# Two query blocks multiplied tile by tile at a kernel's start, with their weights loaded in another order

## The chip, the cores and the metric

The kernel runs on one core of a Trainium2 chip. The time is the device time of one execution in microseconds (us). The engines are TensorE (PE, matrix products), VectorE (DVE), ScalarE (ACT), GpSimd (POOL) and SyncE (SP, which issues the loads). Each works through its own instructions in order and waits for the others by semaphores.

## The reference

Two layers of a small transformer on 512 tokens with 1024 features, in float32. Only the beginning of the first layer is touched:

```python
a = rmsnorm(h, ln_mix_pre[layer])          # h = x at first
mem_n = rmsnorm(mem, ln_mem[layer])
proj = a @ w_in_a[layer]
u = proj[..., :MAIN_WIDTH]                  # 768 columns
v = proj[..., MAIN_WIDTH:2 * MAIN_WIDTH]    # 768 columns
q_mem = proj[..., 2 * MAIN_WIDTH:]          # 256 columns: the query blocks
...
mixed = concatenate([main, memory_attention(q_mem, mem_n, w_mem_kv[layer])], axis=-1)
h = h + rmsnorm(mixed @ w_out[layer], ln_mix_post[layer])
f = rmsnorm(h, ln_ffn_pre[layer])
f = (silu(f @ w_ffn_gate[layer]) * (f @ w_ffn_up[layer])) @ w_ffn_down[layer]
h = h + rmsnorm(f, ln_ffn_post[layer])
```

`rmsnorm(x, g)` divides a token by the root of its mean square and multiplies by the gains g.

## The kernel before

Activations lie with features on the 128 partitions and the 512 tokens along the row, so x is eight tiles, k = 0 to 7, each 128 features x 512 tokens (256 KB). To keep float32 accuracy every operand is cut into two parts: ACT writes a rounded first part ("hi"), DVE the remainder ("lo"), and a product is three matrix products, hi·hi, hi·lo and lo·hi. `split` (line 239) does this for weights, `scaled_parts` (lines 243 and 244) for activations, where it multiplies by the gains as well. `mm3` (lines 191 to 193) issues the three products. The division by the root mean square comes after the products, since it is one number for each token.

`layer_a` opens the program. SP's queue loads weights and x; `query_weights(m, c0, c1)` loads and cuts columns c0 to c1 of query block m's weights (a row of 1024 columns holds the block's eight 128 x 128 tiles, so a half of 512 columns, 256 KB, serves four tiles of x); `tokens(k0, k1)` loads tiles k0 to k1 - 1 of x and cuts them. The query products, two blocks m of 8 tiles with 3 products each, 48 in all, go into one PSUM accumulator for each block (`outs`). They are followed by the products of the first value block (`value_block`, names `v`), whose 128 x 256 accumulators are scaled by `evacuate` (ACT) as they finish.

Beside them runs the mean square: ACT squares each tile (`Norm.add`), DVE adds the squares into `acc`, PE sums over the partitions (`st`, line 288), DVE adds a constant (`var`), POOL takes the power -1/2 (`r`, line 260), and PE spreads it over the partitions (`rb`, line 257), whence DVE copies it to `rbc`. The squares are held back until the last tile of x is cut (`last_a`, `behind`).

Before all this PE runs ten products of zeros (`idle`). The order in which each engine runs the instructions is set by a scheduler from the order of the code and the dependencies; it can move an instruction past others of its engine. SP's loads keep the order of the code. A load also waits until an earlier one, eight before it at most, has landed (its semaphore is used again), and until its buffer is free.

Names in the listings below: `ahi_118`, `alo_119` are the two parts of tile 0 of x, `120`/`121` those of tile 1, and so on to `132`/`133` of tile 7. `ps_183` and `ps_184` are the accumulators of query blocks 0 and 1. `whi`/`wlo` are parts of weights: 138/139 and 160/161 the two halves of block 0; for block 1 they are 155/156 and 175/176 before, 146/147 and 165/166 after; 235 to 250 are value weights.

## Time and profile before

| | us |
|---|---|
| median of 3 runs | 1107.92 (1107.33 to 1109.67) |
| profiled execution | 1106.27 |
| its span, first to last instruction | 1104.4 |
| PE busy in the span | 1096.5 (99%) |
| DVE, ACT, POOL busy | 887.5 (80%), 679.6 (62%), 25.2 (2%) |

The profile comes from one execution. Its timeline lists instructions by engine with their start, duration, line, operation, output and inputs; a bracket at the end names the idle time before an instruction and what ended it. Instructions that follow each other closely can be merged in a row (x2). PE's durations overlap, since products are pipelined, so the distance of two starts tells the rate.

### The profile page before, as it was taken

What the parts mean: (1) busy time and instruction counts of PE and PEld (TensorE: products, weight loads), DVE (VectorE), ACT (ScalarE), POOL (GpSimd) and SP (SyncE); (2) the same over time, 40 slices, a digit from 0 to 9 for tenths busy, and PEclk for the clock granted to TensorE, in tenths of its full rate; (3) what the DMA queues carried; (4) which work ended last, traced back from release to release, by engine and by line L of the source; (5) the groups of instructions that cost most, each with busy time, mean ns of one, the idle gap of its engine ahead of it and who ended that gap; (6) DMA issues with size and microseconds to landing.
All of it is one profiled execution on the core that took longest, in us unless ns stands there. A gap on an engine that the chain in (4) does not pass through costs nothing.

```text
span 1104.4 us, 19436 instructions
## 1 busy us (share of the span) xinstructions
PE 1096.5 (99%) x7332; PEld 998.5 (90%) x7332; DVE 887.5 (80%) x1751; ACT 679.6 (62%) x1426; POOL 25.2 (2%) x41
## 2 busy tenths in 40 slices
PE   9999999999999999999999999999999999999998
PEld 7998889999899899998988998889999899899996
DVE  7879759997698498797968789868998698588776
ACT  7776578664365254477647788868665266255454
POOL 0000000000000000001000000000000000000000
PEclk9999999999999999999999999999999999999999
DMA  7521331334135133245222655531225134233222
GB/s 269 160 79 58 115 115 39 115 115 138 54 115 147 56 104 116 77 154 174 77 77 59 150 129 131 148 115 39 77 91 158 58 114 132 61 114 117 77 96 76
DMA packets 64020, 118.63 MB, mean 107 GB/s; under 512 B 5236, under 2 KB 40072, under 8 KB 63928
## 3 DMA queue, kind: packets, MB, share of 16 engines
q1 hardware_dynamic: 63032, 116.57, 34.8%
q8 instruction: 57, 0.93, 0.4%
q0 software_dynamic: 192, 0.52, 0.2%
q10 hardware_dynamic: 704, 0.32, 0.1%
q14 instruction: 35, 0.29, 0.1%
HBM read 105.23 MB, written 2.10 MB: 97 GB/s over the span
## 4 chain that ended last, share of the span: by engine, by line
PE 93%; ACT 3%; DVE 2%; issue 1%; DMA 0%; SPq 0%; POOLq 0%; POOL 0%; DVEq 0%; ACTq 0%
PE y L191 10%; PE y L192 10%; PE y L193 10%; PE a L191 5%; PE a L193 5%; PE a L192 5%; PE ps L191 4%; PE ps L192 4%; PE ps L193 4%; PE e L191 3%; PE e L193 3%; PE e L192 3%; PE x L193 3%; PE x L191 3%; PE x L192 3%; PE v L191 2%
## 5 line engine op out<-in xcount | busy, mean ns | idle before, releaser
L239 ACT CAST whi<-raw 128x512 fp32r<-128x512 f32 x460 | 277.4, 620 | 262.1 <-PE y L193 118.5
L239 DVE TENSOR_TENSOR wlo<-raw,whi 128x512 fp32r<-128x512 f32 x460 | 307.2, 689 | 112.4 <-ACT whi L239 110.3
L191 PE MATMUL y<-whi,fhi 128*128 128x512 f32 (+1 forms) x356 | 139.6, 393 | 0.0
L193 PE MATMUL y<-whi,flo 128*128 128x512 f32 (+1 forms) x356 | 139.4, 391 | 0.0
L192 PE MATMUL y<-wlo,fhi 128*128 128x512 f32 (+1 forms) x356 | 139.3, 391 | 0.0
L193 PE MATMUL x<-xshi,wlo 128*128 128x256 f32 x320 | 89.8, 281 | 0.0
L191 PE MATMUL x<-xshi,whi 128*128 128x256 f32 x320 | 89.7, 280 | 0.0
L191 PE MATMUL a<-xshi,whi 128*128 128x256 f32 x320 | 89.7, 281 | 0.0
L192 PE MATMUL a<-xslo,whi 128*128 128x256 f32 x320 | 89.7, 280 | 0.0
L192 PE MATMUL x<-xslo,whi 128*128 128x256 f32 x320 | 89.7, 280 | 0.0
L193 PE MATMUL a<-xshi,wlo 128*128 128x256 f32 x320 | 89.6, 281 | 0.0
L193 PEld LDWEIGHTS y<-whi,flo 128*128 128x128 f32 x356 | 66.9, 188 | 15.6 <-DVE flo L239 0.2
L192 PEld LDWEIGHTS y<-wlo,fhi 128*128 128x128 f32 x356 | 66.9, 188 | 14.8 <-DVE wlo L239 0.2
L191 PEld LDWEIGHTS y<-whi,fhi 128*128 128x128 f32 x356 | 66.9, 188 | 14.7
L191 PE MATMUL ps<-xshi,whi 128*128 128x256 f32 (+1 forms) x224 | 68.4, 305 | 0.0
L192 PE MATMUL ps<-xslo,whi 128*128 128x256 f32 (+1 forms) x224 | 66.7, 298 | 0.0
L193 PE MATMUL ps<-xshi,wlo 128*128 128x256 f32 (+1 forms) x224 | 66.3, 298 | 0.0
L191 PEld LDWEIGHTS a<-xshi,whi 128*128 128x128 f32 x320 | 60.3, 188 | 0.3
L192 PEld LDWEIGHTS a<-xslo,whi 128*128 128x128 f32 x320 | 60.2, 188 | 0.4
L191 PEld LDWEIGHTS x<-xshi,whi 128*128 128x128 f32 x320 | 60.2, 188 | 0.0
L193 PEld LDWEIGHTS x<-xshi,wlo 128*128 128x128 f32 x320 | 60.2, 188 | 0.0
L193 PEld LDWEIGHTS a<-xshi,wlo 128*128 128x128 f32 x320 | 60.2, 188 | 0.0
(296 smaller groups left out, 3077.5 us busy)
## 6 DMA issues: line engine op xcount, KB each, us to landing
raw<-in_w_gate SPq DMA_DIRECT2D x44, 512.0 KB, 3.6
raw<-in_w_up SPq DMA_DIRECT2D x44, 512.0 KB, 3.6
raw<-in_w_down SPq DMA_DIRECT2D x44, 512.0 KB, 3.9
raw<-in_w_out SPq DMA_DIRECT2D x16, 512.0 KB, 4.4
raw<-in_w_b_q SPq DMA_DIRECT2D x8, 512.0 KB, 4.6
raw<-in_w_a_v SPq DMA_DIRECT2D x6, 512.0 KB, 8.3
raw<-in_w_a_u SPq DMA_DIRECT2D x6, 512.0 KB
raw<-in_w_v SPq DMA_DIRECT2D x6, 512.0 KB, 3.6
```

What stands on the lines that cost most here:

```text
L191: PE.matmul(o, w[0], x[0], start=start, stop=False, skip_group_check=more)
L192: PE.matmul(o, w[0], x[1], start=False, stop=False, skip_group_check=more)
L193: return PE.matmul(o, w[1], x[0], start=False, stop=stop, skip_group_check=more)
L239: last_parts[:] = A.copy(hi, src), (eng or V).tensor_sub(lo, src, hi)
```

## The change

The code loads block 1's first half of weights between tile 0 and tile 1 of x instead of behind tile 3, and both second halves ahead of tiles 4 to 7 (block 1's stood behind tile 7). The products run over the tiles on the outside and the two blocks on the inside, where they ran over halves, then blocks, then the half's four tiles. The three products of a tile and block come in another order: those with the activation's first part come first, and its remainder last.

```diff
         query_weights(0, 0, 512)
-        for k in range(4):
+        tokens(0, 1)
+        query_weights(1, 0, 512)
+        for k in range(1, 4):
             tokens(k, k + 1)
-        query_weights(1, 0, 512)
-        query_weights(0, 512, 1024)
+        for m in range(2):
+            query_weights(m, 512, 1024)
         tokens(4, 6)
         tokens(6, 8)
         last_a = tuple(last_parts)
-        query_weights(1, 512, 1024)
...
             outs = [ps(t) for t in ("mm", "lg")]
-            for half in range(0, KT, 4):
+            for k in range(KT):
                 for o, w in zip(outs, wq):
-                    for k in range(half, half + 4):
-                        mm3(o, w[k], a[k], k == 0, k == KT - 1)
+                    PE.matmul(o, w[k][0], a[k][0], start=k == 0, stop=False)
+                    PE.matmul(o, w[k][1], a[k][0], start=False, stop=False)
+                    PE.matmul(o, w[k][0], a[k][1], start=False, stop=k == KT - 1)
```

The numbers of instructions on each engine stay the same. PE's order differs from before among the 48 query products and at one place behind them, ACT's and DVE's in the first 60 instructions or so, SP's in the first eight; everything later stands in the order of before.

PE, the first twelve query products, before:

```order
L191 MATMUL ps_183<-ahi_118,whi_138 128x512
L192 MATMUL ps_183<-alo_119,whi_138 128x512
L193 MATMUL ps_183<-ahi_118,wlo_139 128x512
L191 MATMUL ps_183<-ahi_120,whi_138 128x512
L192 MATMUL ps_183<-alo_121,whi_138 128x512
L193 MATMUL ps_183<-ahi_120,wlo_139 128x512
L191 MATMUL ps_183<-ahi_122,whi_138 128x512
L192 MATMUL ps_183<-alo_123,whi_138 128x512
L193 MATMUL ps_183<-ahi_122,wlo_139 128x512
L191 MATMUL ps_183<-ahi_124,whi_138 128x512
L191 MATMUL ps_184<-ahi_118,whi_155 128x512
L192 MATMUL ps_183<-alo_125,whi_138 128x512
```

PE at the same place now:

```order
L672 MATMUL ps_183<-ahi_118,whi_138 128x512
L673 MATMUL ps_183<-ahi_118,wlo_139 128x512
L672 MATMUL ps_184<-ahi_118,whi_146 128x512
L674 MATMUL ps_183<-alo_119,whi_138 128x512
L672 MATMUL ps_183<-ahi_120,whi_138 128x512
L673 MATMUL ps_184<-ahi_118,wlo_147 128x512
L674 MATMUL ps_184<-alo_119,whi_146 128x512
L673 MATMUL ps_183<-ahi_120,wlo_139 128x512
L674 MATMUL ps_183<-alo_121,whi_138 128x512
L672 MATMUL ps_184<-ahi_120,whi_146 128x512
L673 MATMUL ps_184<-ahi_120,wlo_147 128x512
L674 MATMUL ps_184<-alo_121,whi_146 128x512
```

The twelve products took tiles 0 to 3 for block 0 and one of block 1; now they are all of tiles 0 and 1, for both blocks, and the third of them needs block 1's weights.

ACT, from its first cut on, before (135 and 136 are the raw weights of blocks 0 and 1):

```order
L239 CAST whi_138<-raw_135 128x512
L243 ACTIVATE ahi_118<-h,gains 128x512
L243 ACTIVATE ahi_120<-h,gains 128x512
L243 ACTIVATE ahi_122<-h,gains 128x512
L243 ACTIVATE ahi_124<-h,gains 128x512
L239 CAST whi_155<-raw_136 128x512
L239 CAST whi_160<-raw_135 128x512
L243 ACTIVATE ahi_126<-h,gains 128x512
L243 ACTIVATE ahi_128<-h,gains 128x512
L243 ACTIVATE ahi_130<-h,gains 128x512
L243 ACTIVATE ahi_132<-h,gains 128x512
L239 CAST whi_175<-raw_136 128x512
```

ACT at the same place now:

```order
L239 CAST whi_138<-raw_135 128x512
L243 ACTIVATE ahi_118<-h,gains 128x512
L239 CAST whi_146<-raw_136 128x512
L243 ACTIVATE ahi_120<-h,gains 128x512
L243 ACTIVATE ahi_122<-h,gains 128x512
L243 ACTIVATE ahi_124<-h,gains 128x512
L239 CAST whi_160<-raw_135 128x512
L239 CAST whi_165<-raw_136 128x512
L243 ACTIVATE ahi_126<-h,gains 128x512
L243 ACTIVATE ahi_128<-h,gains 128x512
L243 ACTIVATE ahi_130<-h,gains 128x512
L243 ACTIVATE ahi_132<-h,gains 128x512
```

The cut of block 1's first half moved ahead of tiles 1 to 3, that of its second half ahead of tiles 4 to 7. DVE's remainders follow in the same order.

PE in the second value tile (`v_301`), around the sums of squares `st_314`, before:

```order
L192 MATMUL v_301<-wlo_246,ahi_128 128x256
L288 MATMUL st_314<-avg,acc_266 128x1 x4
L193 MATMUL v_301<-whi_245,alo_129 128x256
L191 MATMUL v_301<-whi_249,ahi_130 128x256
L192 MATMUL v_301<-wlo_250,ahi_130 128x256
L193 MATMUL v_301<-whi_249,alo_131 128x256
L191 MATMUL v_301<-whi_249,ahi_132 128x256
L192 MATMUL v_301<-wlo_250,ahi_132 128x256
```

PE at the same place now:

```order
L192 MATMUL v_301<-wlo_246,ahi_128 128x256
L193 MATMUL v_301<-whi_245,alo_129 128x256
L191 MATMUL v_301<-whi_249,ahi_130 128x256
L192 MATMUL v_301<-wlo_250,ahi_130 128x256
L193 MATMUL v_301<-whi_249,alo_131 128x256
L191 MATMUL v_301<-whi_249,ahi_132 128x256
L192 MATMUL v_301<-wlo_250,ahi_132 128x256
L288 MATMUL st_314<-avg,acc_266 128x1 x4
```

The sums moved behind six value products; the spread `rb` twelve and more products further on kept its place.

## The prediction

> **What bounds the kernel now.** I read the page's first lines, then the waits of TensorE (PE) after the opening, then the opening itself, engine by engine, in the timeline. All times are microseconds from the span's start.

> ```profile
> span 1104.4 us, 19436 instructions
> PE 1096.5 (99%) x7332; PEld 998.5 (90%) x7332; DVE 887.5 (80%) x1751; ACT 679.6 (62%) x1426; POOL 25.2 (2%) x41
> ```

> PE is busy in 99% of the span. Busy alone says little, so the next view lists what PE waited for from 18 us to the end (releaser, us in total, times, longest):

> ```profile
> PE o L532 <- ACT pT L239: 0.5, 1, 0.5
> PE yt L881 <- ACT yg L866: 0.2, 1, 0.2
> PE mo L493 <- DVE pT L239: 0.2, 1, 0.2
> PE tr L464 <- DVE p L457: 0.2, 1, 0.2
> PE o L532 <- DVE pT L239: 0.2, 1, 0.2
> ```

> These are all of them: 1.3 us in 1086. After the opening PE never waits for a load, so a shift of PE's stream at 18 us goes through to the end nearly one to one. What the change can win or lose is therefore decided before the first value product. PE's opening:

> ```profile
> 1.26 4.45 PE L89 MATMUL idle<-zeros 128*128 128x512 bf16 x10 [1.26 <-DVE zeros L81]
> 5.78 0.80 PE L191 MATMUL ps<-ahi,whi 128*128 128x512 f32 x1
> 6.56 0.60 PE L192 MATMUL ps<-alo,whi 128*128 128x512 f32 x1
> 7.00 0.40 PE L193 MATMUL ps<-ahi,wlo 128*128 128x512 f32 x1
> 7.43 0.50 PE L191 MATMUL ps<-ahi,whi 128*128 128x512 f32 x1
> 8.22 0.50 PE L192 MATMUL ps<-alo,whi 128*128 128x512 f32 x1 [0.28 <-DVE alo L244]
> 8.55 0.40 PE L193 MATMUL ps<-ahi,wlo 128*128 128x512 f32 x1
> 8.79 0.39 PE L191 MATMUL ps<-ahi,whi 128*128 128x512 f32 x1
> 9.11 0.50 PE L192 MATMUL ps<-alo,whi 128*128 128x512 f32 x1
> 9.45 0.39 PE L193 MATMUL ps<-ahi,wlo 128*128 128x512 f32 x1
> 9.68 0.63 PE L191 MATMUL ps<-ahi,whi 128*128 128x512 f32 x2
> 10.14 0.40 PE L192 MATMUL ps<-alo,whi 128*128 128x512 f32 x1
> 18.76 0.28 PE L191 MATMUL v<-whi,ahi 128*128 128x256 f32 x1
> 18.88 0.28 PE L192 MATMUL v<-wlo,ahi 128*128 128x256 f32 x1
> ```

> The first column is the start. The 48 query products begin at 5.78; the twelfth starts at 10.14, and the first value product at 18.76, so the last 37 run without a gap at (18.76 - 10.14) / 37 = 0.233 us each. Without any wait 48 of them would take 11.18 us and end at 16.96: the opening holds 1.8 us of waiting and slow running, which is 0.16% of the time. No rearrangement of these 48 products alone can win more than that. A change of 0.2%, 2.2 us, is about what a measurement of this kernel tells from none.

> **What the opening waits for.** ScalarE (ACT) makes the first part of each tile; its rows, with the wait in brackets:

> ```profile
> 4.41 0.62 ACT L239 CAST whi<-raw 128x512 fp32r<-128x512 f32 x1 [1.67 <-DMA raw<-in_w_a_q]
> 5.00 0.72 ACT L243 ACTIVATE ahi<-h,gains 128x512 fp32r<-128x512 f32 x1
> 6.65 0.72 ACT L243 ACTIVATE ahi<-h,gains 128x512 fp32r<-128x512 f32 x1 [0.93 <-DMA h<-in_x]
> 7.55 1.38 ACT L243 ACTIVATE ahi<-h,gains 128x512 fp32r<-128x512 f32 x2 [0.17 <-DMA h<-in_x]
> 8.88 1.28 ACT L239 CAST whi<-raw 128x512 fp32r<-128x512 f32 x2
> 10.79 1.34 ACT L243 ACTIVATE ahi<-h,gains 128x512 fp32r<-128x512 f32 x2 [0.64 <-DMA h<-in_x]
> 12.49 1.34 ACT L243 ACTIVATE ahi<-h,gains 128x512 fp32r<-128x512 f32 x2 [0.36 <-DMA h<-in_x]
> 13.73 0.60 ACT L239 CAST whi<-raw 128x512 fp32r<-128x512 f32 x1
> 7.41 2.31 DVE L244 SCALAR_TENSOR_TENSOR alo<-h,gains,ahi 128x512 fp32r<-128x512 f32 x3 [0.90 <-ACT ahi L243]
> 1.00:5.00 4.00, 3.74 (x9) 1.35 (x10) 1.20 (x6) 2.07 (x3) 1.12 (x3) 1.00 0.76 215
> 5.00:10.00 5.00, 4.61 (x13) 2.11 (x12) 3.89 (x6) 3.86 (x7) 0.00 (x0) 1.00 0.95 333
> 10.00:15.00 5.00, 5.00 (x23) 4.04 (x22) 4.42 (x8) 4.01 (x8) 0.00 (x0) 1.00 1.01 395
> ```

> The loads come in the order of SP's queue. Tile 0 is there by 5.00, tile 1 lands at 6.65, tile 2 at 7.55, tile 3 by 8.2 (the pair at 7.55 has no gap), the two halves of weights by 8.88 and 9.5, tiles 4-5 at 10.79, tiles 6-7 at 12.49. The last three rows are stretches of the span, which end in granted clock, DMA share and GB/s. From 10 to 15 us the share is 1.01 at 395 GB/s: the loads are the limit, and a 256 KB piece put ahead of others delays them by 262 KB / 395 GB/s = 0.66 us.

> **The change part by part.** *Block 1's first half (256 KB) goes from sixth place in the queue to third.* Pieces of the same size change places: I give the half tile 1's landing, 6.65, tile 1 that of tile 2, 7.55, tile 2 that of tile 3, 8.2. ACT then cuts the half from 6.65 to 7.27, tile 1 from 7.55 to 8.27; VectorE (DVE) follows 0.75 us behind (three in 2.31), tile 1 done at about 9.05.

> *PE's order.* The first two products (tile 0, both parts of block 0's weights) can run at 5.78 and 6.21. The third needs the half's first part: 7.33, with the 0.06 us that lay between ACT's end (7.37) and PE (7.43) for tile 1. The fourth follows; the fifth needs tile 1's first part, 8.33; the sixth to eighth follow at the 0.23 to 0.33 us of the rows 8.22 to 8.79, to 9.05; the ninth needs tile 1's remainder, ready at 9.12. I put the ninth at 9.28. From there 40 products x 0.233 = 9.33 us: the value products start at 18.61, against 18.76: **-0.15 us**. The saved waits for tiles 2 and 3 are paid by the longer wait for the half and for tile 1: one tile now gives six products, but arrives a place later. If tile 1 came as early as before, the ninth would start at 8.25 and the sum would be -1.2 us; if the half and tile 1 came a further 0.66 us late, the ninth would start at 9.94 and it would be +0.5. I take the middle, since the places are of equal size.

> *Both second halves go ahead of tiles 4 to 7* (one was there already, the other moves past two loads of 512 KB on SP's queue). Tiles 4-5 land 0.66 us later, 11.45, and tiles 6-7 at 13.15. The second cut's 0.62 us on ACT fits into the wait for tiles 4-5 (0.64 before, longer now); without that cover it would delay them 0.62 us. PE asks for tile 4 at product 25: 9.28 + 16 x 0.233 = 13.01, and ACT has it at 11.45 + 0.72 = 12.17. For tile 6, product 37, it is 15.81 against 13.9. Both are hidden, by 0.8 and 1.9 us: 0. The cut at 13.73 is gone, so ACT starts the squares right after tile 7, at 13.15 + 1.34 = 14.5, instead of after that cut, at 14.3: the last add comes about 0.2 us later. No other loads, GpSimd work or instruction counts change; the order beyond 40 us is the same.

> *The column sums move on PE*, by six value products, as the rows of the part on the change show; the diff doesn't say it. What hangs on them:

> ```profile
> 19.04 4.88 DVE L277 TENSOR_TENSOR acc<-acc,sq 128x512 f32<-128x512 f32 x7
> 23.62 0.95 PE L288 MATMUL st<-avg,acc 128*128 128x1 f32 x8
> 24.61 0.16 DVE L291 TENSOR_SCALAR var<-st 128x4 f32<-128x4 f32 x1 [0.68 <-PE st L288]
> 24.85 1.41 POOL L260 TENSOR_TENSOR r<-var,mhalf 128x4 f32<-128x4 f32 x1 [21.92 <-DVE var L291]
> 26.29 0.84 ACT L641 ACTIVATE vg<-v,r 128x256 f32<-128x256 f32 x2 [1.96 <-POOL r L260]
> 26.77 0.60 PE L257 MATMUL rb<-ident,r 128*128 128x128 f32 x4
> ```

> The sums (st) go through DVE (var) and GpSimd (r), and the next step on PE is the spread of r (rb), whose place stays. r is there at 26.29 and PE reaches rb at 26.77, so rb has 0.48 us to spare. Six products at 0.12 us (18.76 to 18.88) are 0.71 us: st starts at 23.62 + 0.71 - 0.15 = 24.18 and r comes at 26.85, while PE, 0.15 us ahead, is at rb at 26.62. **PE waits 0.23 us, +0.25 with the step to PE.** It is bounded by 0 (if the rough GpSimd row is too long) and the whole 0.71. The values' evacuation by ACT at 26.29 waits for r too and comes 0.6 us later; PE's fourth value tile, which takes its buffer, starts twelve products after rb, at 26.77 + 0.36 + 12 x 0.12 = 28.6, and the first evacuation is done by 27.3: covered. The sixth add of squares in the row at 19.04 ends by 23.2, 0.2 us later now, and st starts at 24.18, so the sums are not late.

> Sum: -0.15 + 0.25 = +0.1 us. The profiled execution took 1106.27 around its span of 1104.4, 1.65 below the median of the runs, 1107.92; on the median the sum gives **1108.0**.

> **The rivals.** *The lead is kept.* Tile 1 lands as early as it did, or rb doesn't wait: -0.15 to -1.2 us, 1106.7 to 1107.8. For it: tile 0 was in long before PE began, so loads may not land strictly in their places. Against: tile 1's row shows a true wait of 0.93 us for a queue that now has one more piece ahead.

> *PE stays at its slow rate for longer, and the kernel gets slower.* Up to 7.43 products are 0.43 us apart (7.00 to 7.43, and the ten idle ones, 4.45 / 10), from 8.55 on 0.24, with the granted clock at 1.00 in all three stretches. So some 7 us of nearly gapless work came before the fast rate. After the change PE has a gap from 6.6 to 7.33, and another to 8.33. Before it had gaps of about 0.35 at 6.21 and 7.86, and the fast rate came all the same. If the longer gap makes PE start over and takes as long again, it is slow until 14.3: of the 44 products from 8.33 on, 14 run at 0.43 and 30 at 0.233, the value products start at 21.3, and with rb's 0.25 it is +2.8 us, 1110.7. The point of decision for 0.2% is a slow rate to about 12.9. [...]

> *Tiles 4-5 come later than PE asks for them.* It takes more than 0.8 us beyond the 0.66; each microsecond more costs one. If the second half's move delays them twice as much as its size and their cut queues behind its own, 11.45 + 0.66 + 0.62 + 0.72 = 13.45 against 13.01: +0.45 and the sum, 1108.5.

> **How the numbers follow.** Forecast (within 0.6 us of 1108.0) 0.58; lead kept 0.22; slow rate 0.14, of which 0.06 beyond 2.2 us; late tiles 0.06. The runs before lie between 1107.33 and 1109.67, so scatter alone can carry a result past 0.2%: I give it 0.05 on the faster side, for which the 1.8 us of the opening leave no room, and 0.03 on the slower, which with the 0.06 of the slow rate makes 0.09. Within 0.2% are the remaining 0.86. The range takes in the lead kept and half of the slow rate's 2.8 us, with 0.3 us of scatter at either end: 1106.4 to 1109.7.

> **What would show it.** In the new profile: block 1's first cut starts near 6.65 on ACT and tile 1's near 7.55; the third query product near 7.33 and the ninth near 9.3, all 0.233 us apart from there; no wait at tiles 4 to 7; value products from about 18.6; rb with a wait of some 0.2 us on GpSimd. The prediction is wrong if products stay 0.43 us apart beyond 9 us, if tile 1 lands before 7 us, or if PE waits anywhere that is not named here.

## The result, and the profile after

The changed kernel took 1108.99 us (median of 22 runs, 1106.80 to 1110.43), the kernel before 1107.30 beside it (22 runs, 1105.28 to 1109.67). The ratio is 1.0018, 95% interval 1.0013 to 1.0024: slower by 0.18%, 2.0 us (1.4 to 2.7). By the medians alone it is 1.7 us. That is inside the bound of 0.2% that the prediction called no change, and inside its range, but 1.0 us above its number and clear of zero.

The profiled execution took 1108.57 us. The head of its page:

```profile
span 1106.5 us, 19437 instructions
PE 1095.6 (99%) x7332; PEld 998.8 (90%) x7332; DVE 888.2 (80%) x1751; ACT 679.3 (61%) x1426; POOL 25.4 (2%) x41
```

The span is 2.1 us longer. PE's opening, from its timeline (start, duration, and in brackets the wait and its releaser):

```profile
5.58 0.50 PE L672 MATMUL ps<-ahi,whi 128*128 128x512 f32 x1 [0.48 <-ACT ahi L243]
5.92 0.40 PE L673 MATMUL ps<-ahi,wlo 128*128 128x512 f32 x1
7.28 0.50 PE L672 MATMUL ps<-ahi,whi 128*128 128x512 f32 x1 [0.97 <-ACT whi L239]
...
9.19 0.50 PE L672 MATMUL ps<-ahi,whi 128*128 128x512 f32 x1 [1.18 <-ACT ahi L243]
9.52 0.40 PE L673 MATMUL ps<-ahi,wlo 128*128 128x512 f32 x1
...
10.22 0.40 PE L674 MATMUL ps<-alo,whi 128*128 128x512 f32 x1
...
19.54 0.28 PE L191 MATMUL v<-whi,ahi 128*128 128x256 f32 x1
```

The third product starts at 7.28 (7.33 was forecast), the fifth at 9.19 (8.33) and the ninth at 10.22 (9.28). Behind it 40 products run 0.233 us apart, and the value products start at 19.54, 0.78 us later than before. ACT's rows of the same timeline say which load it was:

```profile
6.61 0.62 ACT L239 CAST whi<-raw 128x512 fp32r<-128x512 f32 x1 [1.08 <-DMA raw<-in_w_a_q]
8.41 1.99 ACT L243 ACTIVATE ahi<-h,gains 128x512 fp32r<-128x512 f32 x3 [1.19 <-DMA h<-in_x]
...
12.29 2.61 ACT L243 ACTIVATE ahi<-h,gains 128x512 fp32r<-128x512 f32 x4 [0.65 <-DMA h<-in_x]
```

Block 1's half was there at 6.61, as forecast (6.65); tile 1, the fourth load, came at 8.41, where the load in fourth place had come at 7.55 before. Tiles 4 and 5 came at 12.29 and PE didn't wait for them. Then the sums, from the timeline of all engines:

```profile
25.08 0.95 PE L288 MATMUL st<-avg,acc 128*128 128x1 f32 x8
...
26.31 1.41 POOL L260 TENSOR_TENSOR r<-var,mhalf 128x4 f32<-128x4 f32 x1 [23.38 <-DVE var L291]
...
27.41 0.27 PE L193 MATMUL v<-whi,alo 128*128 128x256 f32 x1
27.77 0.65 PE L257 MATMUL rb<-ident,r 128*128 128x128 f32 x4
```

The spread rb starts 0.36 us after the product ahead of it, where products are 0.12 apart: a wait of 0.24 us, until r is there (26.31 + 1.41 = 27.72). rb stands 1.00 us later than before. Of PE's waits behind 18 us (total, number, longest) the first of these two has grown, from 0.2 us in one wait before:

```profile
PE o L532 <- DVE pT L239: 0.7, 2, 0.5
PE o L532 <- ACT pT L239: 0.5, 1, 0.5
```

### The profile page after: what moved, and what is told of

Read it like the earlier page. It is cut to its first block, busy times and chain, and to the rows that moved or that the text cites. A ratio compares the mean times of both kernels' runs of the same rounds, so it can differ in the third digit from the quotient of the medians.

```text
span 1106.5 us, 19437 instructions
## 1 busy us (share of the span) xinstructions
PE 1095.6 (99%) x7332; PEld 998.8 (90%) x7332; DVE 888.2 (80%) x1751; ACT 679.3 (61%) x1426; POOL 25.4 (2%) x41
## 4 chain that ended last, share of the span: by engine, by line
PE 91%; ACT 3%; DVE 3%; issue 1%; DMA 1%; SPq 0%; POOL 0%; POOLq 0%; DVEq 0%; ACTq 0%
PE y L191 10%; PE y L193 10%; PE y L192 10%; PE a L191 5%; PE a L193 5%; PE a L192 5%; PE ps L191 4%; PE ps L193 4%; PE ps L192 4%; PE x L191 3%; PE e L193 3%; PE x L193 3%; PE e L191 3%; PE x L192 3%; PE e L192 3%; PE v L191 2%
## 5 line engine op out<-in xcount | busy, mean ns | idle before, releaser
L239 ACT CAST whi<-raw 128x512 fp32r<-128x512 f32 x460 | 277.4, 620 | 262.7 <-PE y L193 118.3
L239 DVE TENSOR_TENSOR wlo<-raw,whi 128x512 fp32r<-128x512 f32 x460 | 307.0, 687 | 115.0 <-ACT whi L239 112.8
L193 PE MATMUL y<-whi,flo 128*128 128x512 f32 (+1 forms) x356 | 139.4, 392 | 0.0
L191 PE MATMUL y<-whi,fhi 128*128 128x512 f32 (+1 forms) x356 | 139.4, 392 | 0.0
L192 PE MATMUL y<-wlo,fhi 128*128 128x512 f32 (+1 forms) x356 | 139.1, 391 | 0.0
L191 PE MATMUL x<-xshi,whi 128*128 128x256 f32 x320 | 89.9, 281 | 0.0
L191 PE MATMUL a<-xshi,whi 128*128 128x256 f32 x320 | 89.9, 281 | 0.0
L192 PE MATMUL a<-xslo,whi 128*128 128x256 f32 x320 | 89.8, 281 | 0.0
L192 PE MATMUL x<-xslo,whi 128*128 128x256 f32 x320 | 89.8, 281 | 0.0
L193 PE MATMUL x<-xshi,wlo 128*128 128x256 f32 x320 | 89.8, 281 | 0.0
L193 PE MATMUL a<-xshi,wlo 128*128 128x256 f32 x320 | 89.7, 281 | 0.0
L193 PEld LDWEIGHTS y<-whi,flo 128*128 128x128 f32 x356 | 66.9, 188 | 15.3 <-DVE flo L239 0.2
L192 PEld LDWEIGHTS y<-wlo,fhi 128*128 128x128 f32 x356 | 66.8, 188 | 14.9 <-DVE wlo L239 0.2
L191 PEld LDWEIGHTS y<-whi,fhi 128*128 128x128 f32 x356 | 66.9, 188 | 14.6
L191 PE MATMUL ps<-xshi,whi 128*128 128x256 f32 (+1 forms) x224 | 68.5, 306 | 0.0
L192 PE MATMUL ps<-xslo,whi 128*128 128x256 f32 (+1 forms) x224 | 66.6, 297 | 0.0
L193 PE MATMUL ps<-xshi,wlo 128*128 128x256 f32 (+1 forms) x224 | 66.3, 297 | 0.0
L192 PEld LDWEIGHTS a<-xslo,whi 128*128 128x128 f32 x320 | 60.3, 188 | 0.4
L191 PEld LDWEIGHTS a<-xshi,whi 128*128 128x128 f32 x320 | 60.2, 188 | 0.3
L192 PEld LDWEIGHTS x<-xslo,whi 128*128 128x128 f32 x320 | 60.3, 188 | 0.0
L193 PEld LDWEIGHTS x<-xshi,wlo 128*128 128x128 f32 x320 | 60.3, 188 | 0.0
L193 PEld LDWEIGHTS a<-xshi,wlo 128*128 128x128 f32 x320 | 60.2, 188 | 0.0
```

The source lines that it names most:

```text
L191: PE.matmul(o, w[0], x[0], start=start, stop=False, skip_group_check=more)
L192: PE.matmul(o, w[0], x[1], start=False, stop=False, skip_group_check=more)
L193: return PE.matmul(o, w[1], x[0], start=False, stop=stop, skip_group_check=more)
L239: last_parts[:] = A.copy(hi, src), (eng or V).tensor_sub(lo, src, hi)
```

## The experiments

Theories at the start: **place** (tile 1 one place later in the queue sets PE's opening), **clock** (PE's gaps hold up the fast rate or end it), and **chance** (landing times vary from one execution to the next). In the table "fourth" is the start of ACT's cut of the fourth load, "value" the start of the first value product, from each kernel's one profile. The column of falls counts the timed executions whose mean granted clock was 0.998 or less; what this says is told below. Of before it takes the 82 executions beside the experiments; those of the first comparison have no clock on record.

| kernel | fourth | value | value - fourth | falls | time against before (95%) |
|---|---|---|---|---|---|
| before | 7.55 | 18.76 | 11.21 | 11 of 82 | |
| before, again | 7.40 | 18.61 | 11.21 | 0 of 1 | one run |
| changed loop, loads of before | 8.04 | 19.16 | 11.12 | 0 of 11 | 0.9994 (0.9985 to 1.0003) |
| the same, again | 7.36 | 18.48 | 11.12 | 1 of 11 | 0.9996 (0.9987 to 1.0005) |
| changed | 8.41 | 19.54 | 11.13 | 15 of 22 | 1.0018 (1.0013 to 1.0024) |
| changed, again | 8.05 | 20.73 | 12.68 | 1 of 1 | one run |
| changed, third | 8.16 | 19.29 | 11.13 | 4 of 11 | 1.0017 (1.0008 to 1.0026) |
| changed loads, loop of before | 8.01 | 19.15 | 11.14 | 6 of 11 | 1.0017 (1.0008 to 1.0026) |
| half behind tile 1 | 8.28 | 19.35 | 11.07 | 2 of 11 | 1.0008 (1.0000 to 1.0017) |
| both halves first | 7.57 | 18.56 | 10.99 | 1 of 11 | 1.0004 (0.9995 to 1.0012) |
| sums early | 7.51 | 18.64 | 11.13 | 4 of 11 | 1.0013 (1.0004 to 1.0022) |
| gaps filled | 7.92 | 19.66 | 11.74 | 1 of 11 | 1.0009 (1.0001 to 1.0018) |
| 18 idle products | 8.24 | 19.22 | 10.98 | 0 of 11 | 1.0005 (0.9997 to 1.0014) |
| 4 idle products | 7.93 | 20.58 | 12.65 | 0 of 6 | 1.0029 (1.0016 to 1.0041) |

**Second profiles of both kernels.** No edit. Before:

> The kernel before once more, for a second profile. If the landing times of the first loads belong to the queue's order, the fourth load (tile 2) is whole within 0.2 us of 7.5 us and the value products start at 18.6 to 18.9 us. If they are chance, tile 2 lands anywhere from 7.2 to 8.5 us and the value products move with it by up to 0.8 us. The moment at which PE's products change from 0.43 to 0.233 us should differ from the first profile's (6.8 us) if it isn't tied to the program.

Changed:

> The changed kernel once more. Place in the queue as the cause: tile 1 lands at 8.2 to 8.5 us again and the value products start at 19.3 to 19.7 us. Chance as the cause: tile 1 lands near 7.6 us and the value products start at 18.6 to 18.9 us, as was predicted. Slow clock as the cause: if the fast rate comes only after PE's gaps, the products from the fifth on are 0.43 us apart and the value products start after 20.5 us.

Before repeated itself: tile 2's cut at 7.40, value products at 18.61 (the fast rate began at 6.16 us instead of 6.80). The changed kernel's tile 1 was late again (8.05, a little earlier than expected), so that was not one bad draw; but the value products came at 20.73, and here the clock is the reason. PE's timeline in this second profile:

```profile
5.54 0.61 PE L672 MATMUL ps<-ahi,whi 128*128 128x512 f32 x1
...
6.75 0.50 PE L672 MATMUL ps<-ahi,whi 128*128 128x512 f32 x1 [0.38 <-ACT whi L239]
...
8.82 0.50 PE L672 MATMUL ps<-ahi,whi 128*128 128x512 f32 x1 [1.34 <-ACT ahi L243]
9.16 0.59 PE L673 MATMUL ps<-ahi,wlo 128*128 128x512 f32 x1
9.55 0.63 PE L674 MATMUL ps<-alo,whi 128*128 128x512 f32 x1
9.97 0.63 PE L673 MATMUL ps<-ahi,wlo 128*128 128x512 f32 x1
...
12.11 0.63 PE L672 MATMUL ps<-ahi,whi 128*128 128x512 f32 x1
12.53 0.44 PE L673 MATMUL ps<-ahi,wlo 128*128 128x512 f32 x1
12.81 0.40 PE L674 MATMUL ps<-alo,whi 128*128 128x512 f32 x1
```

The two gaps over (0.38 and 1.34 us in brackets), products run 0.43 us apart from 9.55 to 12.53, then faster again. Two stretches of the same execution, from the view by stretches (busy time of PE, PEld, DVE, ACT and POOL; the last three columns are granted clock, DMA share and GB/s):

```profile
5.78:9.19 3.41, 1.70 (x6) 0.79 (x7) 1.57 (x3) 1.76 (x3) 0.00 (x0) 1.00 0.98 312
9.19:12.61 3.42, 3.42 (x10) 2.64 (x9) 3.23 (x6) 2.60 (x5) 0.00 (x0) 0.50 1.03 383
```

The clock was granted fully at 5.78, went to half at 9.19 and back at 12.61. In the stretch before the fall PE was busy 1.70 of 3.41 us. The price is 12.68 - 11.13 = 1.55 us. The expectation had one point wrong: the fast rate did not come late, it was lost again.

**The half one place later.**

```diff
         tokens(0, 1)
+        tokens(1, 2)
         query_weights(1, 0, 512)
-        for k in range(1, 4):
+        for k in range(2, 4):
```

> The changed kernel with block 1's first half one place later, behind tile 1. Place as the cause: tile 1 lands at 6.65 us again, five products of block 0 are done before the half comes, the sixth starts at 8.2 to 9.1 us and the value products at 18.2 to 19.1 us, 0.4 to 1.3 us earlier than in the changed kernel; with the wait at the spread of r the time is within -0.05 and +0.06% of before. The products' order as the cause: no gain over the changed kernel, about +0.18%.

Tile 1 came at 5.68, but now the half is fourth, at 8.28, and the value products start at 19.35, later than expected. PE's timeline shows why:

```profile
6.86 0.39 PE L674 MATMUL ps<-ahi,wlo 128*128 128x512 f32 x1
8.95 0.50 PE L673 MATMUL ps<-ahi,whi 128*128 128x512 f32 x1 [1.70 <-ACT whi L239]
```

The first is the fifth product, the second the sixth, which waits 1.70 us for the half. In both orders the piece in fourth place is the one that PE waits for longest. The time, +0.08%, lies between the two kernels and above what place had promised.

**One part at a time.** The loads of the change with the loop of before, then the changed loop with the loads of before (twice):

> The changed order of loads with the products in the code's order of before (halves, then blocks, then tiles). Place as the cause: tile 1 lands at 8.2 to 8.5 us, value products at 19.2 to 19.8 us, time +0.10 to +0.18%. The products' order as the cause: value products at 18.6 to 18.9 us and a time within 0.05% of before.

> The order of loads of before, with the changed loop over the products (tiles outside, blocks inside, remainder last). Loads as the cause: tile 2, fourth in the queue, lands at 7.3 to 7.6 us as in both profiles of before, value products start at 18.5 to 18.9 us, and the time is within 0.05% of before. The products' order as the cause: about +0.18%, as the changed kernel.

> The order of loads of before with the changed loop once more, to see whether its -0.06% was more than scatter: below -0.03% with an interval under zero if it is faster than before, within 0.05% of before if not. The value products should start 11.1 to 11.3 us after the fourth load's landing, as in every profile in which the fast rate held.

The loads alone cost as much as the whole change (+0.17%); the loop alone costs nothing (0.9994 and 0.9996, neither interval clear of 1). So the loss hangs on the order of the loads. (The column sums don't stand alike in these kernels: 45 value products are ahead of them with the loads alone and 42 with the loop alone, against 41 before and 47 in the changed kernel, and the spread rb waits 0.02 us and not at all. The loads alone cost as much without that wait.) How the loss builds up over the kernel is shown further below. But the place theory's reason didn't hold: with the loads of before the fourth cut came at 8.04 in one profile, and with the changed loads at 7.51 in another (sums early). In four profiles with the loads of before it starts at 7.59 us on average, in eight with the changed loads at 8.03; each group has a member that would fit the other. That weights between tiles delay it by 0.4 us is likely from this, not shown.

**Both halves first.**

```diff
-        query_weights(0, 0, 512)
-        tokens(0, 1)
-        query_weights(1, 0, 512)
-        for k in range(1, 4):
+        for m in range(2):
+            query_weights(m, 0, 512)
+        for k in range(4):
```

> The changed kernel with block 1's first half second in the queue, ahead of tile 0, so that both blocks' weights come first and the tiles 0 to 3 follow one another. If a piece's place in the queue alone sets its landing, tile 0 lands at 5.6 to 6.6 us, tile 1 at 8.0 to 8.4 us as in the changed kernel, and value products start at 19.2 to 19.7 us. If putting weights between tiles is what holds the queue up, tile 1 lands at 7.3 to 7.6 us, as the fourth piece did in before, and the value products start at 18.5 to 18.8 us.

7.57 and 18.56: the second case, with a time that can't be told from before's. With one profile, and the scatter just named, it does not prove the second case's reason.

**The sums.** The column sums are held ahead of the next products (and so stand eleven products earlier):

```diff
-                    PE.matmul(st[:, tb : tb + 1], sq, avg, start=n == 0, stop=n == len(some) - 1)
+                    self.end = PE.matmul(st[:, tb : tb + 1], sq, avg, start=n == 0, stop=n == len(some) - 1)
...
-            pieces(2)
+            with behind([pre.end]):
+                pieces(2)
```

> The changed kernel with the column sums of the squares held ahead of the second half of the second value tile, eleven products earlier on PE. As the prediction's step says: no wait at the spread of r, which then follows the products at 0.12 us, and 0.25 us (0.02%) less than the changed kernel, so about +0.16%. If something else held the spread, it waits as before. Tile 1 lands at 8.0 to 8.5 us as in the changed kernel.

The timeline of all engines:

```profile
23.33 1.05 PE L288 MATMUL st<-avg,acc 128*128 128x1 f32 x8 [0.28 <-DVE acc L277]
...
24.67 1.41 POOL L260 TENSOR_TENSOR r<-var,mhalf 128x4 f32<-128x4 f32 x1 [21.74 <-DVE var L291]
...
27.02 0.28 PE L193 MATMUL v<-whi,alo 128*128 128x256 f32 x1
27.14 0.49 PE L257 MATMUL rb<-ident,r 128*128 128x128 f32 x3
```

rb now follows at 0.12 us: the wait was the sums' place, as predicted. But the sums came 0.28 us too early for DVE's last add here, and PE waited that long at st instead: the wait was moved, not saved. The time is +0.13%, which the intervals don't part from +0.17%.

**The clock.** Three kernels with other numbers of zero products: seven more in PE's gaps, 18 at the start instead of 10, and 4 at the start.

```diff
-                    PE.matmul(o, w[k][0], a[k][1], start=False, stop=k == KT - 1)
+                    end = PE.matmul(o, w[k][0], a[k][1], start=False, stop=k == KT - 1)
+                    if k == 0:
+                        idle(2 if o is outs[0] else 5, zero, end)
...
-    idle(10, zero)
+    idle(18, zero)
...
-    idle(10, zero)
+    idle(4, zero)
```

> The changed kernel with seven more products of zeros on PE: two after tile 0's products with block 0, five after those with block 1. They stand in the gaps in which PE waits for tile 1; their sums are thrown away. As built, the column sums also stand earlier on PE, so that the spread of r need not wait (0.25 us). Slow clock as a cause: the rate never falls back after the first rise, so the slowest executions are gone and the time is 0.3 to 0.8 us (0.03 to 0.07%) below the changed kernel's +0.18% on top of the 0.25 us, so +0.08 to +0.13%. Clock without weight on average: +0.14 to +0.17%.

> The changed kernel with 18 products of zeros at the start instead of 10. They keep PE busy to 6.6 to 7.5 us, ahead of the first gap; the ninth query product, which waits for tile 1, should not be later for it. As built, the column sums stand nine products earlier on PE as well (0.25 us). Slow clock as a cause: the rate rises once and stays, the value products start 11.1 to 11.4 us after the fourth load, and the time is +0.06 to +0.13%, about 0.05% or more under the changed kernel beyond the column sums' 0.02%. Without weight of the clock: +0.14 to +0.18%.

> The changed kernel with 4 products of zeros at the start instead of 10 and everything else in the same order, so that PE has its gaps before it has been busy for long. Slow clock as a cause: the fast rate begins only after 10 us, at one of the steps of 3.4 us, the value products start 13 to 14 us after the fourth load's landing, and the time is +0.25 to +0.40%. Without weight of the clock: as the changed kernel, +0.18%.

> The changed kernel a third time, timed beside the other runs of this batch. If its loss is real and not a matter of the chip, +0.13 to +0.24% again. In the profile, the fast rate holds if it began before about 4.6 or after about 6.4 us, and falls back 3.4 us after its beginning if it began between, as in the second profile (5.78, back at 9.19); the value products start 11.15 us after the fourth load's landing where it holds, and 12.7 us after it where it falls back.

The third profile of the changed kernel rose late and held, value products 11.13 us after the fourth cut, and the loss was there again, +0.17%. With 18 idle products PE has one short gap left, by its timeline:

```profile
1.25 5.98 PE L89 MATMUL idle<-zeros 128*128 128x512 bf16 x18 [1.25 <-DVE zeros L81]
6.88 0.59 PE L672 MATMUL ps<-ahi,whi 128*128 128x512 f32 x1
...
9.01 0.50 PE L672 MATMUL ps<-ahi,whi 128*128 128x512 f32 x1 [0.38 <-ACT ahi L243]
...
19.22 0.28 PE L191 MATMUL v<-whi,ahi 128*128 128x256 f32 x1
```

Its time is +0.05% (-0.03 to +0.14), slightly better than expected, and its eleven runs lie between 1106.78 and 1108.17, where those of the changed kernel in the same comparison spread from 1106.84 to 1109.96. So the query products' late start (6.88 instead of 5.58) cost nothing, and the slowest executions are gone. (The sums' earlier place has little part in it: rb doesn't wait, but st starts 0.34 us behind the product ahead of it, where 0.12 is the distance without a wait.)

Each timed execution has its mean granted clock, and this counts the falls. A fall of 3.41 us to half rate, as in the changed kernel's second profile, takes 0.0015 of the mean. In every one of the fourteen profiles the clock also goes to half once at the end, behind PE's last product and 0.1 to 3.3 us before the end of the span, which takes up to another 0.0015. So 0.999 or 1.000 is counted as no fall and 0.998 or less as one (0.996, in three executions, would be more than one). In the second profile of the changed kernel, the one with a fall, it is 0.997; in the thirteen others it is 0.999 or 1.000. Where in the kernel a fall lies, the number doesn't say. At 0.998 or below lie 20 of the 34 executions of the changed kernel, 6 of 11 with the loads alone, 1 of 22 with the loop alone, 11 of 82 of before. With PE's gaps filled it is 1 of 11, and with 18 idle products, which leave only the gap of 0.38, none of 11. These kernels differ only at their start, so the falls that come and go with the gaps are put down to the opening: the gaps end the fast rate, and filling them keeps it. **Clock** holds. The length of the gaps alone doesn't decide. One gap of 1.70 us, as with the half behind tile 1, goes with 2 falls in 11; the changed kernel's make 2.15, 1.72 and 1.48 us in its three profiles, and only the second has a fall. The expectation of the third profile put the fall at a first rise between 4.6 and 6.4 us. These limits were the author's estimate, and no run shows them: the first rise lay at 5.78 in the profile with the fall, at 4.36 and 7.05 in the two without. With a fall were 20 of 34 executions, 59%. In the comparison of the third profile the changed kernel took 1109.5 us on average with a fall and 1107.8 without, before 1106.85 without; in the comparison of the result the changed kernel's averages are 1109.3 and 1107.9. A fall goes with 1.4 to 1.7 us, and 1.0 us is lost without one. For the loop alone that second part is nothing (1106.6 in its first comparison, before 1106.65).

PE's timeline with 4 idle products:

```profile
1.25 1.89 PE L89 MATMUL idle<-zeros 128*128 128x512 bf16 x4 [1.25 <-DVE zeros L81]
5.58 0.79 PE L672 MATMUL ps<-ahi,whi 128*128 128x512 f32 x1 [2.44 <-ACT ahi L243]
...
11.47 0.63 PE L673 MATMUL ps<-ahi,wlo 128*128 128x512 f32 x1
11.90 0.46 PE L674 MATMUL ps<-alo,whi 128*128 128x512 f32 x1
12.19 0.40 PE L672 MATMUL ps<-ahi,whi 128*128 128x512 f32 x1
```

The distance of two products falls from 0.43 to 0.29 at 11.90, so the fast rate begins at about 12.0; the value products start 12.65 us after the fourth cut (13 to 14 were expected), and the time is +0.29%. The column of falls counts none for it, since there was no fast rate to lose. Filling the gaps themselves cost 0.6 us in the opening (11.74) and still brought the time down to +0.09%, at the lower end of what the clock theory said.

No kernel here beats before beyond its interval; the loop with the loads of before comes nearest.

## Why the prediction was right, and which steps failed

The forecast of no change and the range held; the sum had 0.1 of 2.0 us. That the change stayed under 0.2% is in good part luck: 0.18%, with an interval up to 0.24%, is what terms that the sum put at nothing happened to add up to. Two of the prediction's own signs of being wrong came, products 0.43 us apart beyond 9 us (in one of three profiles) and a wait of PE that it hadn't named. And its 1108.0 was built on a median of three runs of before, 1107.92, which lies 0.6 above the 1107.30 of the 22 runs.

The table shows where the time came from: how much later than in the first profile of before the same product starts (median of those within 8 us), worked out from the starts of some 7300 products that both traces hold; the numbers are good to about 0.04. The middle columns are the steps between such places, in us.

| kernel | at 30 us | 30 to 600 | 600 to 660 | 660 to 1085 | at 1085 us |
|---|---|---|---|---|---|
| before, again | -0.15 | -0.20 | -0.17 | -0.05 | -0.57 |
| changed loop, loads of before | 0.39 | -0.34 | +0.13 | +0.47 | 0.65 |
| the same, again | -0.28 | -0.38 | +0.09 | +0.46 | -0.11 |
| changed | 1.02 | -0.82 | +0.70 | +1.15 | 2.05 |
| changed, again | 2.22 | -0.84 | +1.14 | +1.12 | 3.64 |
| changed, third | 0.77 | -0.55 | +1.10 | +1.18 | 2.50 |
| changed loads, loop of before | 0.47 | -0.42 | +0.96 | +1.27 | 2.28 |
| half behind tile 1 | 0.83 | -0.84 | -0.19 | +1.08 | 0.88 |
| both halves first | -0.17 | -0.23 | +0.46 | +1.23 | 1.29 |
| sums early | 0.33 | -0.82 | -0.17 | +1.15 | 0.49 |
| gaps filled | 0.82 | -0.82 | +0.55 | +1.19 | 1.75 |
| 18 idle products | 0.72 | -0.85 | +0.40 | +1.12 | 1.39 |
| 4 idle products | 2.05 | -0.83 | +0.98 | +1.19 | 3.39 |

In the first profile, half of the changed kernel's 2.05 us is the opening with the spread, of which the prediction had 0.1; the other half comes behind it, where it had nothing. This first profile of before is an early one, 1.0 us below the median of its runs, and the changed kernel's first profile has no fall. So the 2.05 us fit the 1.0 us that is lost without a fall; the falls come on top. By the prediction's steps:

*What bounds the kernel.* That PE sets the end, so that a shift at the spread stays, holds from 30 to 100 us (1.02 and 0.93). That nothing else would shift it later was wrong, as the last two points show.

*The half and tile 1: -0.15 us.* This step failed, by the landing it was built on. Tile 1 was given the fourth place's 7.55; it came at 8.41, 8.05 and 8.16. The working behind it was sound: the ninth product comes 10.22 - 8.41 = 1.81 us after the cut, 40 products x 0.233 = 9.32 follow, 11.13 in all, and 11.13 again in the third profile (12.68 in the second, where the rate fell). Before, the eighth product came at 9.11, 1.56 us after tile 2's cut, and 40 x 0.233 stood behind the next one: 11.2. The trade "one tile for six products, a place later" is even, as was said; what is not even is when the fourth load lands. The rival by which the lead is kept fell as well, since tile 1 came later than 7.55. Measured +0.78 in the first pair of profiles, of which 0.86 is the landing.

*Second halves ahead of tiles 4 to 7: 0.* Right: no wait there, though tiles 4 and 5 came at 12.29 instead of 11.45.

*The column sums: +0.25.* Right, 0.24 us, and in its place.

*The slow rate, a rival with 0.14.* It was thought too rare and priced too high. It struck 20 of 34 executions, at 1.4 to 1.7 us (1.55 in the opening of the one profile that shows it), beside the 2.55 (2.8 less rb's 0.25) that a slow rate "as long again" would have cost. On the average of the executions, by 0.59 x 1.4 to 1.7, less 0.13 x 1.5 for the falls of before, that makes 0.6 to 0.8 us, which with the 1.0 lost without a fall is the 1.7 between the medians. Part of the price came from a row misread: the product at 7.43 came 0.43 us behind that at 7.00 because tile 1's first part was ready only at 7.37, not because PE was slow (the product at 7.00 lasts 0.40 us, that at 6.56 lasts 0.60). The clock in that trace rises at 6.80, so 5.5 us of work from 1.26 on came before the fast rate, not 7, and "as long again" was priced too long. "Before had gaps of about 0.35, and the fast rate came all the same" was the right row, but it says nothing of gaps of 1.5 to 2.2 us together: in the second profile gaps of 1.72 us left PE busy for 1.70 of the 3.41 us before the fall.

*Not foreseen: a wait at 645 us, +0.7 to +1.1.* In all three profiles of the changed kernel PE waits about 0.5 us longer at `o`. The rows lead back to a copy from buffer to buffer on SP's queue (qa<-whi): ACT waits until it has landed before it cuts the next queries into `whi`, and DVE and PE follow. The copy's issue and ACT's cut, from the timelines of all engines, before and then changed, and PE's row in the timeline of the changed kernel:

```profile
630.73 0.51 SPq L1345 DMA_DIRECT2D qa<-whi  x1
634.86 0.62 ACT L239 CAST whi<-q 128x512 fp32r<-128x512 f32 x1 [0.78 <-DMA qa<-whi]
```

```profile
630.94 0.51 SPq L1347 DMA_DIRECT2D qa<-whi  x1
635.76 0.62 ACT L239 CAST whi<-q 128x512 fp32r<-128x512 f32 x1 [1.48 <-DMA qa<-whi]
```

```profile
645.42 0.50 PE L532 MATMUL o<-pT,vals 128*128 128x512 f32 x1 [0.55 <-DVE pT L239]
```

From issue to cut it is 4.13 us before and 4.82 in the changed kernel, 0.69 more, which is the table's step. In its other two profiles it is 5.23 and 5.22, with the loads alone 5.04, with the loop alone 4.31 and 4.26; wherever it is above 4.13, the excess is the step of the table to within 0.06. With the changed loads it can also be shorter (3.45 with the half behind tile 1; no wait at all with the sums early), and then the step is -0.2. SP itself waits longer too, for a block of output weights (1.7 us instead of 1.2), but only behind this copy's issue, so that wait isn't the cause. Why the copy lands later is open; it was not tried by itself.

*Not foreseen: another distance of products, -0.8 and +1.15.* Between 30 and 600 us and between 660 and 1085 us no single step carries the shift (the largest are two of 0.12 at 237 us); it grows evenly. In the second stretch 160 products x<-xshi,whi of the changed kernel follow 0.20 us later in all than before, 1.2 ns each at 0.117 us. It isn't scatter: the two profiles of the changed loop agree to 0.04 us in both stretches, and the ten profiles with reordered loads in the table all have +1.08 to +1.27 in the second. So it belongs to the kernel as built, though the order there is the same. What makes it is open. In sum it is +0.3 us for the changed kernel and +0.85 for the loads alone.

## What to carry to other kernels

When loads and products are reordered at a kernel's start, count for each place in the queue how many products may run before the next landing, and look at the gaps that this leaves on TensorE: here gaps of 1.5 to 2.2 us together, worth next to nothing in the sum, went with a fall from the fast rate in 20 of 34 executions, at 1.4 to 1.7 us each, and with the gaps filled in 1 of 11. One profile is one draw of landing times and of the clock (in the changed kernel's three, tile 1 came at 8.41, 8.05 and 8.16 us, and the clock first rose at 4.36, 5.78 and 7.05): the mean granted clock of every timed execution, and a kernel with filler products in the gap, tell a cause from a draw. And a change's time should be followed along the whole kernel by the starts of the same products, since half of this one's lay far from the edit.

## What the runs showed of the hardware

```profile
4.36:7.77 3.41, 1.96 (x8) 0.70 (x6) 1.96 (x3) 1.69 (x3) 0.00 (x0) 1.00 0.83 229
```

In the thirteen profiles without a fall the 3.41 us behind the first rise hold 1.94 us of PE's work or more (1.94 in the changed kernel's third). So the one fall in an opening came behind 1.70 us of work, and none behind 1.94 or more; what lies between, no profile shows. And the granted clock reads 1.00 before the first rise too, as in the kernel with 4 idle products, where products are 0.43 us apart nearly through this whole stretch:

```profile
8.62:12.03 3.41, 3.41 (x10) 2.64 (x9) 3.34 (x6) 2.73 (x6) 0.00 (x0) 1.00 1.03 395
```

In this opening the distance of two products tells the rate, not that column.
